# A two-layer encoder trunk on one core: the first norm's scale and offset as rows spread by products, the first loads in another order, and clears on GpSimd

## The chip, the cores and the metric

The kernel runs on one core of one Trainium2 chip, in one launch. The metric is device time in microseconds (us) of that launch, the median of several runs. The engines go by the profile's names: PE (TensorE, with PEld for its weight loads), DVE (VectorE), ACT (ScalarE), POOL (GpSimd) and SP (SyncE, which here only issues DMAs). Each engine takes its own instructions strictly in order and waits on semaphores where an instruction needs another engine's result.

## The reference, cut to what matters

```python
def layer_norm(x, g, b):
    mu = jnp.mean(x, axis=-1, keepdims=True)
    var = jnp.mean(jnp.square(x - mu), axis=-1, keepdims=True)
    return (x - mu) * lax.rsqrt(var + LN_EPS) * g + b

def reference(x, p, ln0_g, ln0_b, w_in, ...):       # x: (1, 512, 1024)
    h = layer_norm(x, ln0_g, ln0_b)                 # the first norm
    for i in range(2):
        u = h @ w_in[i]                             # 1024 -> 2560 columns
        y_hy = hyena_mixer(u[..., :768], ...)       # long convolution
        y_att = diff_attention(u[..., 768:1280], u[..., 1280:1792], u[..., 1792:2304], ...)
        y_pool = pool_mixer(u[..., 2304:], ...)
        mix = jnp.concatenate([y_hy, y_att, y_pool], axis=-1) @ w_out[i]
        h = layer_norm(DN_ALPHA * h + mix, ln1_g[i], ln1_b[i])
        y_moe = hier_moe(h, ...)                    # 16 experts, 2 of them per token
        y_ple = jax.nn.sigmoid(h @ ple_wg[i] + ple_bg[i]) * (p[i] @ ple_wp[i])
        h = layer_norm(DN_ALPHA * h + y_moe + y_ple, ln2_g[i], ln2_b[i])
    return h
```

Only the first norm, the first columns of the first input projection (the query, key and value of attention head 0) and what is loaded or cleared beside them are touched by the change.

## The kernel before, in words

The 512 tokens are four tiles `h[0]` to `h[3]` of 128 tokens by 1024 columns. A tile is normalised in place (`ln`: two passes on DVE, the first subtracts the mean and multiplies by the scale `gb[0]`, the second multiplies by the inverse deviation and adds the offset `gb[1]`), transposed on PE against an identity matrix (`transpose_hl`, eight products `tr` of 128 columns, four to a PSUM bank) and split into a high and a low part, `hT[0]` cast on ACT and `hT[1]` subtracted on DVE (`split`). Weights come from memory as tiles `raw` and are split in the same way into `whi` (ACT) and `wlo` (DVE). Each float32 product is then three PE products, high by high, low by high and high by low (`mm3`, the lines L218 to L220).

The work is written as a list of units (`add`), each with its DMAs, a shape and a generator of PE work. `pump` issues the DMAs of units up to some number ahead and the splits up to another. Units 0 to 3 are the four quarters of attention head 0's weights (`add_head(i, 0, before=...)`); the fourth one's generator runs, tile by tile, norm, transposes and all 24 products `pj` of that tile, then copies the result out of PSUM on ACT (`head_evac`: `uqk`, `uv`). Units 4 and up are the Hyena weights, 512 KB each.

The statistics of tile 0 are taken on DVE (`bn_stats`). Those of tiles 1 to 3 are taken on ACT (`moments`): two passes `lnsq` that sum a half each (L359), a small DVE step `lnneg`, and one pass that squares and sums (L364), after which POOL makes the inverse deviation `lnrs` in two small steps. The first norm pass of a tile overwrites what the squaring pass reads, so it waits for that pass.

The order on each engine is made by a recording layer that places instructions when it expects their inputs; `issue_after(x)` keeps what is issued under it behind instruction `x`, and `behind()` keeps it behind the last norm. Up to eight DMAs of SP are under way at once: the ninth waits for the first.

Of the kernel before, what the change touches and what calls it, by code (L numbers as in the profile page):

```python
# [9 lines left out]
F32 = mybir.dt.float32  # L10
F32R = mybir.dt.float32r
BF16 = mybir.dt.bfloat16
# [9 lines left out]
NT = 4  # L22
# [22 lines left out]
C_N = 818  # L45
# [98 lines left out]
def flat(t):  # L144
    n = len(t.shape) - 1
    if n == 1:
        return t
    letters = " ".join("abcdef"[:n])
    return t.rearrange(f"p {letters} -> p ({letters})")


class Trunk:
# [68 lines left out]

    def split(self, hi, lo, src):

        self.nc.scalar.copy(hi, src)  # L224
        self.nc.vector.tensor_sub(lo, src, hi.bitcast(F32))  # L225


# [160 lines left out]
    def setup(self):  # L388
        nc, A = self.nc, self.A
        cst = self.cst  # L390
        self.ident = cst[:, C_ID:C_ID + 128]
        self.alt = cst[:, C_ALT:C_ALT + 258]
        self.cos = cst[:, C_COS:C_COS + 64].rearrange("p (t d) -> p t d", t=NT)
        self.sin = cst[:, C_SIN:C_SIN + 64].rearrange("p (t d) -> p t d", t=NT)
        self.iota = cst[:, C_IOTA:C_IOTA + 128]
        self.mhalf = self.cp.tile([128, NT], F32, name="mhalf")
        nc.gpsimd.memset(self.mhalf, -0.5)
        self.ones = self.cp.tile([128, 128], F32, name="ones")
        nc.vector.memset(self.ones, 1.0)
        self.tri_b = self.cp.tile([128, 128], BF16, name="tri_b")  # L400
        nc.vector.tensor_copy(self.tri_b, cst[:, C_TRI:C_TRI + 128])
        self.ones_b = self.cp.tile([128, 128], BF16, name="ones_b")
        nc.vector.memset(self.ones_b, 1.0)

        self.qL = self.cp.tile([128, 2, 512], F32R, name="qL")
        nc.vector.memset(flat(self.qL).bitcast(F32), 0.0)

    def setup_late(self):
        nc, A = self.nc, self.A

        vr = self.s2([128, 128], "vr")
        for name, rows in VEC:
            src = A[name]
            nc.sync.dma_start(vr[VOFF[name]:VOFF[name] + rows],
                              bass.AP(tensor=src.tensor, offset=src.offset, ap=[[128, rows], [1, 128]]))
        ps = self.ps("vps")
        nc.tensor.transpose(ps[:, :NVEC], vr[:NVEC], self.ident[:NVEC, :NVEC])
        self.vec = self.cp.tile([128, NVEC], F32, name="vec")
        nc.vector.tensor_copy(self.vec, ps[:, :NVEC])

        self.pw = self.cp.tile([128, DEPTH * 2, 128], F32, name="pw")
        nc.vector.memset(self.pw, 0.0)
        for half in range(2):
            src = A["pool_w"]
            nc.sync.dma_start(
                self.pw[half * 64:half * 64 + 64, :, half * 64:half * 64 + 64],
                bass.AP(tensor=src.tensor, offset=src.offset + half * 4096,
                        ap=[[64, 64], [2 * 4096, DEPTH * 2], [1, 64]]))

        for _ in range(2):  # L430
            x = self.xp.tile([128, 1024], F32, name="xe", tag="xe")
            nc.vector.memset(x, 0.0)

    def lam(self):

        nc, A = self.nc, self.A
        lq = self.s2([128, 2, 2, 2, 64], "lq")
        for n, (a, b) in enumerate((("att_lq1", "att_lk1"), ("att_lq2", "att_lk2"))):
            for o, nm in enumerate((a, b)):
                src = A[nm]  # L440
                nc.sync.dma_start(lq[:, :, n, o], bass.AP(tensor=src.tensor, offset=src.offset,
                                                          ap=[[0, 128], [64, DEPTH], [1, 64]]))
        nc.vector.tensor_mul(lq[:, :, :, 0], lq[:, :, :, 0], lq[:, :, :, 1])
        s = self.sm.tile([128, 2, 2], F32, name="lam_s")
        nc.vector.tensor_reduce(s, lq[:, :, :, 0], axis=AX.X, op=OP.add)
        nc.scalar.activation(s, s, AF.Exp)
        self.nlam = self.cp.tile([128, DEPTH], F32, name="nlam")
        nc.vector.tensor_sub(self.nlam, s[:, :, 1], s[:, :, 0])
        for i in range(DEPTH):
            nc.vector.tensor_scalar(self.nlam[:, i:i + 1], self.nlam[:, i:i + 1], -self.lam_init(i), None, op0=OP.add)  # L450
# [294 lines left out]
    def add_head(self, i, j, before=None):  # L745

        w = self.A["w_in"][i]
        st = {"w": []}

        def mms(ps, t, q, wp):  # L750
            for k in range(2):
                self.mm3(ps[:, :384], [x[:, q * 2 + k, t * 128:(t + 1) * 128] for x in self.hT],
                         [x[:, k] for x in wp], q == 0 and k == 0, q == 3 and k == 1)

        def emit(q):
            def f(wp):
                st["w"].append(wp)
                if before is not None:
                    if q < 3:
                        yield 0.01  # L760
                        return
                    self.new_u()
                    before(0)
                    for t in range(NT):
                        self.stream_tile(self.h[t], self.hT, t)
                        if t + 1 < NT:
                            before(t + 1)
                        ps = self.ps("pj")
                        for n, x in enumerate(st["w"]):
                            mms(ps, t, n, x)  # L770
                        self.head_evac(t, ps)

                        yield 15.36 if t == NT - 1 else 0
                    return
                if q == 0:
                    st["ps"] = [self.ps("pj") for _ in range(NT)]
                if q == 3:
                    self.new_u()
                for t in range(NT):
                    mms(st["ps"][t], t, q, wp)  # L780
                    if q == 3:
                        self.head_evac(t, st["ps"][t])
                    yield 0.96
            return f

        for q in range(4):
            srcs = [((lambda r, s=s: r[:, :, s * 128:(s + 1) * 128]),
                     w[q * 256:(q + 1) * 256, 768 + s * 512 + j * 128:768 + s * 512 + (j + 1) * 128]
                     .rearrange("(k p) n -> p k n", p=128)) for s in range(3)]
            self.add(srcs, [2, 384], emit(q))  # L790

    def new_u(self):
# [217 lines left out]
    def gate_weights(self, i):  # L1010
        nc, A = self.nc, self.A
        raw = self.sm.tile([128, 8, 20], F32, name="gwr", bufs=1)
        nc.sync.dma_start(raw[:, :, 0:4], A["moe_wgc"][i].rearrange("(k p) n -> p k n", p=128))
        nc.sync.dma_start(raw[:, :, 4:20], A["moe_wgf"][i].rearrange("(k p) n -> p k n", p=128))
        gb = self.sm.tile([128, 20], F32, name="gb", bufs=1)
        for src, a, n in ((A["moe_bgc"][i], 0, 4), (A["moe_bgf"][i], 4, 16)):
            nc.sync.dma_start(gb[:, a:a + n], self.row_bcast(src, n))
        gw = self.sm.tile([128, 8, 2, 20], F32R, name="gwhl", bufs=1)
        self.split(gw[:, :, 0], gw[:, :, 1], raw)
        self.gate = gw, gb  # L1020

    def logits(self, half):
# [471 lines left out]
    def start_norm(self, i, t):  # L1494
        if i == 0:
            if t == 0:
                self.ln(self.h[0], self.h[0], self.gb, self.ln_stats(self.h[0]), True)
                self.stats = [None] + [self.ln_stats(self.h[u]) for u in range(1, NT)]
            else:
                with self.behind():  # L1500
                    self.ln(self.h[t], self.h[t], self.gb, self.stats[t])
            self.dump(f"h0_{t}", self.h[t])
        else:
            self.finish(i - 1, t)
# [138 lines left out]
    def build(self):  # L1643
        nc, A = self.nc, self.A
        for i in range(DEPTH):
            self.plan(i)
        self.h = []
        for t in range(NT):
            x = self.s4([128, 1024], "h")
            for cs in (slice(0, 512), slice(512, 1024)) if t == 0 else (slice(0, 1024),):  # L1650
                nc.sync.dma_start(x[:, cs], A["x"][0, t * 128:(t + 1) * 128, cs])
            self.h.append(x)
            if t == 0:
                self.gb = self.gain(A["ln0_g"], A["ln0_b"])
                self.cst = self.cp.tile([128, C_N], F32, name="cst")
                nc.sync.dma_start(self.cst, self.C["cst"])
                self.pump(0, -1)
        self.setup()
        self.hT = self.new_hT()
        self.hd = self.dp.tile([S, 1024], F32, name="hd")  # L1660
        self.yd = self.dp.tile([S, 1024], F32, name="yd")
# [38 lines left out]
```

## Time and profile before

| | |
|---|---|
| median of 3 runs | 1043.53 us (1042.79 to 1048.24) |
| the profiled execution's own time | 1045.37 us |
| its span, first to last instruction | 1043.6 us |
| PE busy | 968.6 us, 93% of the span |
| DVE busy | 779.1 us, 75% |
| ACT busy | 613.6 us, 59% |
| POOL busy | 172.9 us, 17% |

The own time is 1.8 us above the span: that is what lies around the first and last instruction. PE is nearly always busy, except at the very start, so a wait of PE in the first 45 us, where all of the change lies, is what matters; idle time on the other engines costs nothing by itself.

### The profile page before, as it was taken

The page shows a single profiled execution, that of the slowest core. Times are in us where ns is not written, and L with a number is a line of the kernel's source. Part 1 is how long each engine was busy: PE and PEld are TensorE (multiplying, and loading weights), DVE is VectorE, ACT ScalarE, POOL GpSimd, SP SyncE. Part 2 cuts the span into 40 slices and gives each one's busy share as a digit, 9 for nine tenths or more (in the row PEclk, how much of TensorE's full clock was granted, in tenths as well). Part 3 has the DMA queues.
Part 4 walks back from the last instruction along what each step waited for, and adds up shares of the span by engine and source line. Part 5 has one row for each costly group of instructions (what it writes and reads, how often), then busy time and mean ns, then how long its engine had stood idle before and what let it go on. Part 6 is the DMA issues. An engine that isn't in the chain of part 4 may idle for free. (4 is left out here: it accounts for less than half of the span.)

```text
span 1043.6 us, 14416 instructions
## 1 busy us (share of the span) xinstructions
PE 968.6 (93%) x4869; PEld 800.6 (77%) x4870; DVE 779.1 (75%) x1301; ACT 613.6 (59%) x1046; POOL 172.9 (17%) x170
## 2 busy tenths in 40 slices
PE   4999999999989999999979999999998999999995
PEld 3887889898767788777758889898776778877762
DVE  7576897777676778887865578847678587888785
ACT  5425464655653768886843346654655386888673
POOL 1101000000222222422121000000012222333121
PEclk9999999999999999999989999999999999999997
DMA  8816121222974999999974412122186399999974
GB/s 262 239 37 142 51 71 52 71 81 68 316 242 102 306 302 311 307 292 301 285 261 114 109 56 67 51 70 83 61 302 243 94 329 302 315 300 312 293 207 161
DMA packets 156010, 197.49 MB, mean 189 GB/s; under 512 B 20296, under 2 KB 123786, under 8 KB 155925
## 3 DMA queue, kind: packets, MB, share of 16 engines
q1 hardware_dynamic: 135253, 155.58, 45.5%
q0 software_dynamic: 20672, 40.87, 15.1%
q8 instruction: 42, 0.69, 0.3%
q14 instruction: 43, 0.35, 0.1%
HBM read 182.85 MB, written 29.36 MB: 203 GB/s over the span
## 5 line engine op out<-in xcount | busy, mean ns | idle before, releaser
L225 DVE TENSOR_TENSOR wlo<-raw,whi 128x1024 fp32r<-128x1024 f32 (+2 forms) x278 | 324.1, 1182 | 66.0 <-ACT whi L224 61.1
L224 ACT CAST whi<-raw 128x1024 fp32r<-128x1024 f32 (+2 forms) x278 | 277.9, 1024 | 33.1 <-DMA raw<-in_moe_w_dram 13.9
L218 PE MATMUL e<-whi,xT 128*128 128x512 f32 x256 | 106.6, 416 | 2.7 <-ACT xT L224 1.8
L219 PE MATMUL e<-wlo,xT 128*128 128x512 f32 x256 | 103.7, 405 | 0.1
L220 PE MATMUL e<-whi,xT 128*128 128x512 f32 x256 | 101.8, 398 | 0.0
L218 PE MATMUL pj<-whi,hT 128*128 128x384 f32 x256 | 90.0, 352 | 2.3 <-ACT hT L224 1.8
L219 PE MATMUL pj<-wlo,hT 128*128 128x384 f32 x256 | 88.2, 345 | 0.3 <-DVE wlo L225 0.3
L220 PE MATMUL pj<-whi,hT 128*128 128x384 f32 x256 | 87.3, 342 | 0.6 <-DVE hT L225 0.5
L1257 POOL DMA_INDIRECT yd<-ye,rt_tok x28 | 53.1, 1895 | 187.2 <-ACT ye L1323 66.7
L868 ACT ACTIVATE prob<-sc,mx 128x512 f32<-128x512 f32 x64 | 43.7, 688 | 39.1 <-DVE mx L867 36.6
L308 POOL TENSOR_TENSOR ors<-rs_y,mhalf 128x4 f32<-128x4 f32 x8 | 8.5, 1057 | 335.3 <-DVE rs_y L307 335.3
L1251 POOL DMA_INDIRECT xe<-hd,rt_tok x32 | 48.8, 1525 | 91.4 <-PE tr L376 48.1
L218 PEld LDWEIGHTS e<-whi,xT 128*128 128x128 f32 x256 | 48.9, 191 | 12.9 <-ACT xT L224 2.2
L219 PEld LDWEIGHTS e<-wlo,xT 128*128 128x128 f32 x256 | 48.8, 191 | 11.4 <-DVE wlo L225 2.4
L220 PEld LDWEIGHTS e<-whi,xT 128*128 128x128 f32 x256 | 48.8, 191 | 10.0
L219 PE MATMUL e<-wlo,actT 128*128 128x512 f32 x128 | 51.6, 403 | 3.1 <-DVE wlo L225 3.1
L218 PE MATMUL mo<-whi,YT 128*128 128x512 f32 x128 | 53.2, 415 | 0.0
L218 PEld LDWEIGHTS pj<-whi,hT 128*128 128x128 f32 x256 | 48.9, 191 | 4.8 <-ACT hT L224 2.5
L219 PE MATMUL pl<-wlo,hT 128*128 128x512 f32 x128 | 51.4, 401 | 1.1 <-DVE wlo L225 1.1
L218 PE MATMUL pl<-whi,hT 128*128 128x512 f32 x128 | 50.8, 402 | 0.6 <-ACT whi L224 0.5
L218 PE MATMUL e<-whi,actT 128*128 128x512 f32 x128 | 47.8, 398 | 3.8 <-ACT whi L224 2.9
L218 PE MATMUL pj<-hT,whi 128*128 128x512 f32 x128 | 51.2, 404 | 0.0
(340 smaller groups left out, 2313.1 us busy)
## 6 DMA issues: line engine op xcount, KB each, us to landing
raw<-in_moe_w_dram SPq DMA_DIRECT2D x256, 256.0 KB
raw<-in_moe_w_dram SPq DMA_DIRECT2D x64, 512.0 KB
raw<-in_w_in_dram SPq DMA_DIRECT2D x96, 128.0 KB
raw<-in_w_in_dram SPq DMA_DIRECT2D x16, 512.0 KB
raw<-in_ple_wg_dram SPq DMA_DIRECT2D x16, 512.0 KB
raw<-in_w_out_dram SPq DMA_DIRECT2D x14, 512.0 KB
tabi<-c_tabi_dram POOLq DMA_DIRECT2D x8, 516.0 KB, 4.6
tabf<-c_tabf_dram POOLq DMA_DIRECT2D x8, 512.0 KB
```

What stands on the lines that cost most here:

```text
L218: mm(ps, a[0], b[0], start=start, stop=False)
L219: mm(ps, a[0], b[1], start=False, stop=False)
L220: mm(ps, a[1], b[0], start=False, stop=stop)
L224: self.nc.scalar.copy(hi, src)
L225: self.nc.vector.tensor_sub(lo, src, hi.bitcast(F32))
L308: nc.gpsimd.tensor_tensor(out, y, self.mhalf[:, :n], op=OP.pow)
L868: nc.scalar.activation(p[:, c], o, AF.Exp, bias=mx[:, c:c + 1], accum_out=sm[:, c:c + 1])
L1251: self.nc.gpsimd.indirect_dma_start(out=x, out_offset=None, in_=self.hd[:, :], in_offset=bass.IndirectOffsetOnAxis(ap=tok, axis=0), bounds ...
L1257: self.nc.gpsimd.indirect_dma_start(out=self.yd[:, :], out_offset=bass.IndirectOffsetOnAxis(ap=row, axis=0), in_=y, in_offset=None, bounds ...
```

## The change

The scale and the offset of the first norm were two DMAs that each wrote one row of 4 KB to all 128 partitions (512 KB). They are now two DMAs of one row into one partition, and a product of a column of ones with that row, 512 columns at a time, spreads it over the partitions in PSUM; ACT copies the four results to two tiles. Of the constants only the identity (64 KB) is loaded at first. The weights of head 0 are eight DMAs of 192 KB in place of twelve of 128 KB, and all eight stand ahead of tiles 1 to 3 of x. The clears of `qL`, `pw` and two tiles `xe` move from DVE to POOL. The statistics of tiles 1 to 3 and the gate weights' split are kept behind the latest weight cast (`self.cast`).

```diff
     def split(self, hi, lo, src):
-        self.nc.scalar.copy(hi, src)
+        self.cast = self.nc.scalar.copy(hi, src).ins
         self.nc.vector.tensor_sub(lo, src, hi.bitcast(F32))
...
-        self.tri_b = self.cp.tile([128, 128], BF16, name="tri_b")
-        nc.vector.tensor_copy(self.tri_b, cst[:, C_TRI:C_TRI + 128])
-        self.ones_b = self.cp.tile([128, 128], BF16, name="ones_b")
-        nc.vector.memset(self.ones_b, 1.0)
...
-        nc.vector.memset(flat(self.qL).bitcast(F32), 0.0)
+        nc.gpsimd.memset(flat(self.qL).bitcast(F32), 0.0)
...
-        nc.vector.memset(self.pw, 0.0)
+        nc.gpsimd.memset(self.pw, 0.0)
...
-            nc.vector.memset(x, 0.0)
+            nc.gpsimd.memset(x, 0.0)
...
     def lam(self):
+        self.tri_b = self.cp.tile([128, 128], BF16, name="tri_b")
+        with self.behind():
+            nc.vector.tensor_copy(self.tri_b, self.cst[:, C_TRI:C_TRI + 128])
+        self.ones_b = self.cp.tile([128, 128], BF16, name="ones_b")
+        nc.vector.memset(self.ones_b, 1.0)
...
         for q in range(4):
-            srcs = [((lambda r, s=s: r[:, :, s * 128:(s + 1) * 128]),
-                     w[q * 256:(q + 1) * 256, 768 + s * 512 + j * 128:768 + s * 512 + (j + 1) * 128]
-                     .rearrange("(k p) n -> p k n", p=128)) for s in range(3)]
+            srcs = [((lambda r, k=k: r[:, k].rearrange("p (s n) -> p s n", s=3)),
+                     w[q * 256 + k * 128:q * 256 + (k + 1) * 128, 768:2304]
+                     .rearrange("p (s n) -> p s n", s=3)[:, :, j * 128:(j + 1) * 128]) for k in range(2)]
...
-        self.split(gw[:, :, 0], gw[:, :, 1], raw)
+        with self.behind(), self.tc.issue_after(self.cast):
+            self.split(gw[:, :, 0], gw[:, :, 1], raw)
...
                 self.ln(self.h[0], self.h[0], self.gb, self.ln_stats(self.h[0]), True)
-                self.stats = [None] + [self.ln_stats(self.h[u]) for u in range(1, NT)]
+                with self.tc.issue_after(self.cast):
+                    self.stats = [None] + [self.ln_stats(self.h[u]) for u in range(1, NT)]
...
             if t == 0:
-                self.gb = self.gain(A["ln0_g"], A["ln0_b"])
-                self.cst = self.cp.tile([128, C_N], F32, name="cst")
-                nc.sync.dma_start(self.cst, self.C["cst"])
-                self.pump(0, -1)
+                for src in (A["ln0_g"], A["ln0_b"]):
+                    r = self.s4([128, 1024], "grow")
+                    nc.sync.dma_start(r[0:1], bass.AP(tensor=src.tensor, offset=src.offset, ap=[[0, 1], [1, 1024]]))
+                    rows.append(r)
+                nc.sync.dma_start(self.cst[:, :128], self.C["cst"][:, :128])
+                self.pump(3, -1)
+        nc.sync.dma_start(self.cst[:, 128:], self.C["cst"][:, 128:])
         self.setup()
+        self.gb = []
+        for r in rows:
+            g = self.s4([128, 1024], "gain")
+            for c in range(2):
+                cs = slice(c * 512, (c + 1) * 512)
+                ps = self.ps("gb")
+                nc.tensor.matmul(ps, self.ones[0:1], r[0:1, cs], start=True, stop=True)
+                nc.scalar.copy(g[:, cs], ps)
+            self.gb.append(g)
```

What stands where on three engines follows. After line 400 the changed kernel's line numbers are shifted a little (L797 is L798, L1651 is L1657).

ACT before, from its first instruction that needs a result: casts of tile 0's transposes (`hT`) and weights (`whi`), and between them the statistics `lnsq` of tiles 1 to 3.

```order
L224 CAST hT_104<-tr 128x4x128
L224 CAST whi<-raw 128x768
L359 ACTIVATE lnsq,lnsum<-h 128x512 x2
L224 CAST hT_104<-tr 128x4x128
L364 ACTIVATE lnsq,lnvar<-h,lnneg 128x1024
L359 ACTIVATE lnsq,lnsum<-h 128x512 x2
L364 ACTIVATE lnsq,lnvar<-h,lnneg 128x1024
L224 CAST whi<-raw 128x768
```

ACT in the changed kernel, from its first copy on; the 128x1024 casts are the Hyena units 4 and 5, `uqk` is the copy of tile 0's finished products out of PSUM.

```order
L1677 COPY gain<-gb 128x512 x4
L224 CAST whi<-raw 128x768 x2
L224 CAST hT_123<-tr 128x4x128
L224 CAST whi<-raw 128x768
L224 CAST hT_123<-tr 128x4x128
L224 CAST whi<-raw 128x768
L224 CAST whi<-raw 128x1024
L359 ACTIVATE lnsq,lnsum<-h 128x512 x2
L798 COPY uqk<-pj 128x256
L224 CAST whi<-raw 128x1024
L364 ACTIVATE lnsq,lnvar<-h,lnneg 128x1024
```

The squaring pass of tile 1 (L364) stood in fifth place, behind one weight cast; it now stands behind all four casts of head 0's weights, both Hyena casts and the copy `uqk` of tile 0.

DVE in the changed kernel around the norm of tile 0 (`h<-h,lnneg,gain` is the first pass, `h<-h,lnrs,gain` a half of the second) and on to the first pass of tile 1. Before, the half passes stood together, with only the cast of `tri_b` between them.

```order
L334 SCALAR_TENSOR_TENSOR h<-h,lnneg,gain 128x1024
L336 SCALAR_TENSOR_TENSOR h<-h,lnrs,gain 128x512
L225 TENSOR_TENSOR wlo<-raw,whi 128x768
L336 SCALAR_TENSOR_TENSOR h<-h,lnrs,gain 128x512
L225 TENSOR_TENSOR wlo<-raw,whi 128x768
L225 TENSOR_TENSOR hT_124<-tr,hT_123 128x4x128
L225 TENSOR_TENSOR wlo<-raw,whi 128x768
```

A weight split now stands between the two halves of tile 0's second pass: the second half waits for what that split waits for, the first weight cast on ACT.

SP in the changed kernel, from its first issue; the tiles are x (`h`), the rows (`grow`), the constants (`cst`) and the weights (`raw`).

```order
L1657 DMA h<-in_x_dram 128x512 x2
L1662 DMA grow<-in_ln_g_dram 1x1024
L1662 DMA grow<-in_ln_b_dram 1x1024
L1664 DMA cst<-c_cst_dram 128x128
L240 DMA raw<-in_w_in_dram 128x3x128 x8
L1657 DMA h<-in_x_dram 128x1024 x3
L1667 DMA cst<-c_cst_dram 128x690
L421 DMA pw<-in_pool_w_dram 64x4x64 x2
L1014 DMA gwr<-in_moe_wgc_dram 128x8x4
L240 DMA raw<-in_w_in_dram 128x4x256
```

Before, the two 512 KB rows and all constants stood in the places of the short rows and the identity, then one unit of weights, then x, then the other three units. The last row here is Hyena unit 4; unit 5 comes four DMAs later.

## Rows read from the trace of the kernel before

**Rows 1.** The page: busy time of PE, share of the span, count.

```profile
PE 968.6 (93%) x4869; PEld 800.6 (77%) x4870; DVE 779.1 (75%) x1301; ACT 613.6 (59%) x1046; POOL 172.9 (17%) x170
```

**Rows 2.** The timeline of PE: start, us, line, out<-in, count, [idle before it <- releaser].

```profile
11.42 1.95 PE L376 MATMUL tr<-cst,h 128*128 128x128 f32 x8 [11.42 <-DMA cst<-c_cst_dram]
...
15.71 0.52 PE L218 MATMUL pj<-whi,hT 128*128 128x384 f32 x1
...
16.35 0.52 PE L220 MATMUL pj<-whi,hT 128*128 128x384 f32 x1
20.20 0.90 PE L376 MATMUL tr<-cst,h 128*128 128x128 f32 x3 [3.33 <-DVE h L336]
...
25.51 0.34 PE L220 MATMUL pj<-whi,hT 128*128 128x384 f32 x1
25.68 0.34 PE L218 MATMUL pj<-whi,hT 128*128 128x384 f32 x1
...
43.04 0.50 PE L218 MATMUL pj<-hT,whi 128*128 128x512 f32 x1
```

**Rows 3.** Windows: stretch, then us and busy (count) by engine, granted clock, DMA.

```profile
43.00:87.00 44.00, 44.00 (x213) 36.29 (x212) 27.86 (x54) 14.93 (x23) 0.33 (x2) 1.00 0.27 77
...
89.50:94.00 4.50, 4.50 (x16) 3.52 (x17) 3.18 (x15) 2.20 (x7) 3.06 (x5) 0.62 0.20 24
```

**Rows 4.** The timeline of DVE.

```profile
4.37 0.69 DVE L321 BATCH_NORM_STATS2 bnst<-h 128x6 f32<-128x512 f32 x1
5.22 0.91 DVE L432 MEMSET xe<- 128x1024 f32 x1 [0.16 <-issue]
...
8.99 1.28 DVE L334 SCALAR_TENSOR_TENSOR h<-h,lnneg,gain 128x1024 f32<-128x1024 f32 x1 [2.60 <-DMA gain<-in_ln_g_dram]
...
11.45 0.75 DVE L336 SCALAR_TENSOR_TENSOR h<-h,lnrs,gain 128x512 f32<-128x512 f32 x1
...
13.89 0.96 DVE L225 TENSOR_TENSOR wlo<-raw,whi 128x768 fp32r<-128x768 f32 x1
...
16.86 1.28 DVE L334 SCALAR_TENSOR_TENSOR h<-h,lnneg,gain 128x1024 f32<-128x1024 f32 x1 [0.45 <-ACT lnsq L364]
```

**Rows 5.** The timeline of ACT.

```profile
12.54 0.59 ACT L224 CAST hT<-tr 128x512 fp32r<-128x512 f32 x1 [10.49 <-PE tr L376]
13.02 0.83 ACT L224 CAST whi<-raw 128x768 fp32r<-128x768 f32 x1
...
15.58 1.15 ACT L364 ACTIVATE lnsq<-h,lnneg 128x1024 bf16<-128x1024 f32 x1
...
28.17 0.38 ACT L797 COPY uqk<-pj 128x256 f32<-128x256 f32 x1 [1.33 <-PE pj L220]
...
28.59 1.06 ACT L224 CAST whi<-raw 128x1024 fp32r<-128x1024 f32 x1
```

**Rows 6.** The timeline of PE: the one full float32 product of 512 columns there.

```profile
135.59 1.03 PE L734 MATMUL pm<-py,pw 128*128 128x512 f32 x2
```

**Rows 7.** DMA packets of 0 to 20 us, of 15 to 17.5, of 12 to 14.

```profile
DMA packets 4698, 5.43 MB, mean 271 GB/s; under 512 B 320, under 2 KB 3674, under 8 KB 4698
...
DMA packets 1197, 0.64 MB, mean 257 GB/s; under 512 B 78, under 2 KB 1178, under 8 KB 1197
...
DMA packets 299, 0.79 MB, mean 394 GB/s; under 512 B 27, under 2 KB 118, under 8 KB 299
```

**Rows 8.** The timeline of PE behind a wait in the middle of the Hyena part.

```profile
89.50 1.20 PE L636 MATMUL edt<-cst,ed 128*128 128x128 f32 x6 [2.26 <-DVE ed L631]
...
91.78 0.63 PE L220 MATMUL pj<-hT,wlo 128*128 128x512 f32 x1
...
94.07 0.39 PE L220 MATMUL pj<-hT,wlo 128*128 128x512 f32 x1
```

**Rows 9.** The timeline of POOL.

```profile
0.76 0.10 POOL L397 MEMSET mhalf<- 128x4 f32 x1 [0.29 <-POOLq L1686]
...
6.57 0.56 POOL L308 TENSOR_TENSOR lnrs<-rs_y,mhalf 128x1 f32<-128x1 f32 x1
```

More of the change, by code (lines that the diff above doesn't have):

```diff
@@ L1647, in build @@
         self.h = []
+        self.cst = self.cp.tile([128, C_N], F32, name="cst")
+        rows = []
         for t in range(NT):
```

## The prediction, made before the changed kernel had run

> **What bounds the kernel now.** I read the page first: PE is busy 93% of the span [rows 1], so the question is where PE waits and whether the change touches such a wait. Then the windows: from 43 us on PE is busy 44.00 of 44.00 us [rows 3], so whatever time the start gives or takes at 43.04, where the first Hyena product begins [rows 2], is handed on in full. Last the timelines up to that point, one engine at a time.
>
> PE has nothing to do until 11.42, when the constants, and with them the identity, have landed. Tile 0's products then start, and the sixth begins at 16.35. At 20.20 PE resumes, after 3.33 us of waiting for tile 1's norm on DVE [rows 2]. The rows also carry a clock. Two products of 384 columns are 0.64 us apart from 15.71 to 16.35, 0.32 each, and only 0.17 from 25.51 to 25.68: first the pace of the 1.2 GHz level, then that of 2.4 [rows 2]. PE had been idle before both slow stretches.
>
> What delays tile 0 is DVE's wait of 2.60 us for the 512 KB scale, to 8.99 [rows 4]. What delays the rest is ACT, which does casts and statistics in one strict order.
>
> **The change, step by step.** Removed: the 1 MB of broadcast rows, most of the constants ahead of the weights, and 3.2 us of clears on DVE (3,584 columns at 0.91 us per 1,024 [rows 4]). The clears are worth nothing by themselves: DVE ended them early enough to wait 2.60 us for the scale.
>
> *The rows.* They stand where the scale stood on SP, behind x's first tile, whose second half DVE reads at 4.37 without a wait [rows 4]. I let them land at 4.4; the bounds are 4.4 (they queue behind that half) and 9.0 (when the scale itself landed).
>
> *The four products.* They are full float32 products of 512 columns. One, as two records, takes 1.03 us from first start to last end [rows 6]. Behind one another I estimate 0.9: 0.17 for 384 columns makes 0.23 for 512, times four. At the slow pace it is 1.8. PE comes to them from idle, so I take three slow and one fast, 6.3 us; the bounds are 3.6 and 7.2. They end at 10.7.
>
> *The second half of tile 0.* The fourth copy takes 0.59, as the cast of the same shape does, the first weight cast 0.83 [rows 5], its `wlo` 0.96, the half pass 0.75 [rows 4]. They stand in one line because DVE's order now puts `wlo` between the two half passes. Half of the 1.95 us of eight transposes follows [rows 2], 1.0. So 10.7 + 0.6 + 0.8 + 1.0 + 0.75 + 1.0 = 14.8 for the start of tile 0's products; before, the last half pass ended at 12.2 [rows 4]. The early identity thus buys nothing, since the spread products take its place on the path.
>
> *Tile 0.* All four quarters of the weights are loaded by then: 1.57 MB at the 257 GB/s of a stretch that moves almost only 512 B packets [rows 7] are 6.1 us, from 4.4 to 10.5. DVE's three further `wlo` (0.96) and two `hT` (taken as the half pass, 0.75) [rows 4] end near 18.2. PE needs 24 products, 4.1 us fast or 7.7 slow; I take 6.0, so tile 0 ends at 20.8. Before, ACT waited for that end until 28.17 [rows 5]: this part is 7 us better.
>
> *Tile 1.* Here the change takes it back. On ACT the copy `uqk` of tile 0 and Hyena unit 5's cast now stand ahead of tile 1's squaring pass, and tile 1's norm waits for that pass, since it writes over what the pass reads (the wait at 16.86) [rows 4]. So 20.8 + 0.38 + 1.06 + 1.15 [rows 5] = 23.4, two passes of 1.28 [rows 4], and PE transposes tile 1 at 26.0, where it was 20.20. PE idles 5 us in between.
>
> *From there to 43.04.* Before it was 22.84 us for 90 of the 96 products. Now 72 are left, 18 × 0.17 = 3.1 less, so 19.7: 26.0 + 19.7 = 45.7. In both PE begins this stretch slow, so that cancels. The sum is 45.7 − 43.04 = **+2.7 us**.
>
> *At nothing, and what covers it.* GpSimd's clears end before the inverse deviation is wanted at 10.4 (below). The late constants: only `tri_b` on DVE reads them, in the slack before tile 1's statistics. Eight weight DMAs for twelve move the same bytes in the same 512 B pieces. The gate weights' split is wanted only behind the attention. The SP queue: `pw` now waits for a clear on POOL, with the gate weights and Hyena units queued behind it, but SP reaches it only near 10, past the clears.
>
> The profiled execution took 1045.37 us, so its like would take 1048.1; the median of the runs is 1.84 lower, 1043.53 + 2.7 = **1046.2 us**. A measurement of this kernel tells about 0.5% (5.2 us) from no change, so that is inside.
>
> **The rivals.**
>
> *A, the forecast: tile 1 comes late* (0.54). Its own range is +1.5 to +5.2, from the slow or fast products (−2.7, +0.9) and tile 0 (−1.9, +1.7), of which the lower end is cut off as under B.
>
> *B, no difference at all* (0.16). If PE ran fast through the spread products and tile 0, that would end at 16.2. But unit 5's cast also needs its data. By the sizes of the tiles about 5.35 MB stand ahead of or in it, and before 5.43 MB had moved by 20.0 us [rows 7]. So its cast starts near 20.2, tile 1 is transposed at 25.0, and the sum is +1.7. Only if PE's clock also stayed up over that wait would 2.5 us more be saved (as much as the slow rows from 20.20 to 25.5 cost over fast ones [rows 2]): −0.8. Against it stands the wait in front of 89.50: after 2.26 us the products took 0.63 us, at the end 0.39 [rows 8], with a granted clock of 0.62 for that stretch [rows 3]. The Trainium skill (TensorE: Matmul & The Clock Gate, Part 1) says that the gate sets the clock by how busy the array has recently been; the trace agrees at 89.50. By the page the early products should help tile 0 and the idle time after it should undo that for tile 1, which is the order of A. The Trainium skill (DMA: Bandwidth & Descriptors, Specifications) calls 512 B enough for line rate; this trace has 257 GB/s with such packets and 394 with mostly 4 KB ones [rows 7], so here it is not. By the page the weights would take 4 us, unit 5's data would come 2 us sooner, and the sum in B would be that much lower.
>
> *C, faster by over 0.5%* (0.05). The start alone can't give it. The wait of 2.26 us before 89.50 and the slow rows after it (4.5 us at 0.62, 1.7 us lost) would have to go as well; with B that makes −0.8 − 4.0 = −4.8, 1038.7 us, and it would take a little more. Against: DVE's work there follows from PE's products, so both shift together.
>
> *D, slower by over 0.5%* (0.25): GpSimd's clears are slow. They run one after another from 0.87, and the two small steps that give tile 0's inverse deviation stand behind them; the second took 0.56 [rows 9], and I estimate 0.8 for both. The half pass wants it at 10.4, so the clears may take 8.7 us, 2.7 times DVE's 3.2. No wide clear on POOL is in the trace; the bounds are 0.10 us each, as for four columns [rows 9], and no upper one. I take DVE's rate, the nearest by size. At four times it, 12.8 us, the deviation would come at 14.4 and everything 4.0 later: +6.7, 1050.2 us. Rows that land as late as the scale did cost 4.6, 1050.8. The Trainium skill (GPSIMD Engine Reference, Elementwise — side-by-side cycle accounting) gives GpSimd 1.96 times VectorE's time for an addition and advises against moving such work there; no run here shows it. By the page the clears would take an estimated 6.3 us, still under 8.7, and the sum would stay.
>
> **How the numbers follow.** Below −5.2 only C counts, 0.05; above +5.2 D, 0.25; the rest, A and B, 0.70. The range leaves out C and the far end of D, somewhat under 2 in 10: 1042.5 (B, less 0.2) to 1051.5 (D at its two prices, and a little over).
>
> **What would show it.** In the changed profile: rows landing (the first spread product) near 4.4; clears on POOL ended by 9.6; four products ended near 10.7; tile 0's first `pj` near 14.8 and `uqk` waiting for PE until about 21; then, the main thing, PE idle some 5 us before tile 1's transposes at about 26, released by DVE's norm, with slow rows after it; the first Hyena product near 45.7. Wrong would be: tile 1's transposes before 22, or fast rows straight after the wait (B or C); a first half pass that waits for POOL (D); or a first Hyena product at 45.7 and a total that doesn't follow it.

## The result, and the profile of the changed kernel

| | before | changed |
|---|---|---|
| median of 20 runs each, taken together | 1043.57 us (1039.58 to 1048.24) | 1049.99 us (1046.09 to 1057.79) |
| ratio of the times | | 1.0070, 95% interval 1.0057 to 1.0084 |
| the profiled execution's own time | 1045.37 us | 1050.24 us |
| its span | 1043.6 us | 1048.5 us |
| first Hyena product | 43.04 us | 47.67 us |

The change makes the kernel slower, by 6.4 us in the medians and 7.3 us (5.9 to 8.8) by the ratio: more than the 0.5% that can be told from no change, and inside the range given (1042.5 to 1051.5), but not the case that was called likeliest.

The page's first line for the changed kernel answers to [rows 1]. PE's share is the same, but it is busy 5.6 us longer, and its idle time is 74.3 us (1048.5 less 974.2) where it was 75.0 (1043.6 less 968.6). So this line shows no added wait; by itself it would put the loss on the spread products, which are new work. Where the time went has to be read from the timelines and the experiments.

```profile
PE 974.2 (93%) x4877; PEld 804.2 (77%) x4878; DVE 776.1 (74%) x1297; ACT 615.7 (59%) x1050; POOL 174.5 (17%) x174
```

The timeline of PE up to the first Hyena product answers to [rows 2].

```profile
4.22 7.16 PE L1676 MATMUL gb<-grow,ones 1*128 1x512 f32 x8 [4.22 <-DMA grow<-in_ln_g_dram]
...
14.44 1.12 PE L376 MATMUL tr<-cst,h 128*128 128x128 f32 x4 [2.02 <-DVE h L336]
15.21 0.67 PE L218 MATMUL pj<-whi,hT 128*128 128x384 f32 x1
...
18.31 0.52 PE L218 MATMUL pj<-whi,hT 128*128 128x384 f32 x1
18.63 0.44 PE L219 MATMUL pj<-wlo,hT 128*128 128x384 f32 x1
18.91 0.34 PE L220 MATMUL pj<-whi,hT 128*128 128x384 f32 x1
...
21.02 0.33 PE L220 MATMUL pj<-whi,hT 128*128 128x384 f32 x1
27.59 1.97 PE L376 MATMUL tr<-cst,h 128*128 128x128 f32 x8 [6.24 <-DVE h L336]
29.38 0.69 PE L218 MATMUL pj<-whi,hT 128*128 128x384 f32 x1
...
47.67 0.50 PE L218 MATMUL pj<-hT,whi 128*128 128x512 f32 x1
```

Read it from the start: the rows land at 4.22 and the spread products take 7.16 us (eight records, two for each of four products). Tile 0's products begin at 15.21, 0.32 apart until 18.63 and 0.17 apart from 18.91 on. They end at 21.35 (21.02 + 0.33), and then PE has nothing for 6.24 us, until DVE has normalised tile 1. Before, that wait was 3.33 us and ended at 20.20 [rows 2]. The spread products fall into time in which PE used to wait for the constants, until 11.42 [rows 2].

ACT's timeline, which answers to [rows 5], says where the wait comes from.

```profile
11.41 0.58 ACT L1677 COPY gain<-gb 128x512 f32<-128x512 f32 x1 [1.12 <-PE gb L1676]
...
19.57 1.05 ACT L224 CAST whi<-raw 128x1024 fp32r<-128x1024 f32 x1 [2.66 <-DMA raw<-in_w_in_dram]
20.52 0.63 ACT L359 ACTIVATE lnsq<-h 128x512 bf16<-128x512 f32 x1
...
21.76 0.35 ACT L798 COPY uqk<-pj 128x256 f32<-128x256 f32 x1
22.03 1.04 ACT L224 CAST whi<-raw 128x1024 fp32r<-128x1024 f32 x1
22.98 1.14 ACT L364 ACTIVATE lnsq<-h,lnneg 128x1024 bf16<-128x1024 f32 x1
```

ACT stands idle for 2.66 us in front of unit 4's cast, whose data are there at 19.57. Tile 1's two sums come only behind that cast, then `uqk` and unit 5's cast, then the squaring pass at 22.98.

DVE and POOL, behind it, answer to [rows 4] and [rows 9].

```profile
24.25 1.28 DVE L334 SCALAR_TENSOR_TENSOR h<-h,lnneg,gain 128x1024 f32<-128x1024 f32 x1 [2.15 <-ACT lnsq L364]
...
26.25 1.28 DVE L336 SCALAR_TENSOR_TENSOR h<-h,lnrs,gain 128x1024 f32<-128x1024 f32 x1 [0.56 <-POOL lnrs L308]
```

```profile
0.80 0.95 POOL L402 MEMSET qL<- 128x1024 f32 x1
1.69 0.52 POOL L418 MEMSET pw<- 128x512 f32 x1
2.15 1.84 POOL L428 MEMSET xe<- 128x1024 f32 x2
5.48 0.19 POOL L305 TENSOR_SCALAR rs_y<-bnmv 128x1 f32<-128x1 f32 x1 [1.48 <-DVE bnmv L323]
...
24.30 1.28 POOL L305 TENSOR_SCALAR rs_y<-lnvar 128x1 f32<-128x1 f32 x1 [18.00 <-ACT lnsq L364]
25.67 0.55 POOL L308 TENSOR_TENSOR lnrs<-rs_y,mhalf 128x1 f32<-128x1 f32 x1
```

The clears are over at 3.99. For tile 1, DVE's second pass waits another 0.56 us for the inverse deviation: the small step `rs_y`, 0.19 us for tile 0, takes 1.28 us while DVE's first pass runs beside it. That wait isn't new. In the kernel before, tile 1's second pass had it too:

```profile
18.86 1.28 DVE L336 SCALAR_TENSOR_TENSOR h<-h,lnrs,gain 128x1024 f32<-128x1024 f32 x1 [0.57 <-POOL lnrs L308]
```

### The profile page after: what moved, and what is told of

It is laid out like the page before. It is cut to its first block, busy times and chain, and to the rows that moved or that the text cites. A ratio compares the mean times of both kernels' runs of the same rounds, so it can differ in the third digit from the quotient of the medians.

```text
span 1048.5 us, 14369 instructions
## 1 busy us (share of the span) xinstructions
PE 974.2 (93%) x4877; PEld 804.2 (77%) x4878; DVE 776.1 (74%) x1297; ACT 615.7 (59%) x1050; POOL 174.5 (17%) x174
## 5 line engine op out<-in xcount | busy, mean ns | idle before, releaser
L224 ACT CAST whi<-raw 128x1024 fp32r<-128x1024 f32 (+2 forms) x278 | 277.3, 1024 | 28.1 <-DMA raw<-in_moe_w_dram 10.2
L1253 POOL DMA_INDIRECT xe<-hd,rt_tok x32 | 46.7, 1459 | 89.8 <-PE tr L376 46.7
L218 PE MATMUL pl<-whi,hT 128*128 128x512 f32 x128 | 51.6, 408 | 1.8 <-ACT whi L224 1.8
L220 PE MATMUL pl<-whi,hT 128*128 128x512 f32 x128 | 51.5, 403 | 0.0
```

Source lines behind the costliest of these rows:

```text
L218: mm(ps, a[0], b[0], start=start, stop=False)
L220: mm(ps, a[1], b[0], start=False, stop=stop)
L224: self.cast = self.nc.scalar.copy(hi, src).ins
L1253: self.nc.gpsimd.indirect_dma_start(out=x, out_offset=None, in_=self.hd[:, :], in_offset=bass.IndirectOffsetOnAxis(ap=tok, axis=0), bounds ...
```

## The experiments

Theory T: tile 1's norm is late because its statistics stand on ACT behind unit 4's cast, with its data, and behind `uqk` and unit 5's cast. Rival R: the four spread products make tile 0 late and all else follows. Rival Q: x's tiles are late because the weights are loaded ahead of them. Theory F, added later, says that small loads delay unit 4's data.

The first four ran side by side (before: 1042.68 us).

**e1, the statistics no longer held back.**

```diff
-                with self.tc.issue_after(self.cast):
+                with contextlib.nullcontext():
                     self.stats = [None] + [self.ln_stats(self.h[u]) for u in range(1, NT)]
```

The new first line is an empty context, which holds nothing back.

> The changed kernel, but the statistics of tiles 1 to 3 are no longer kept behind the latest weight cast; all else as changed. ACT's order then has tile 1's two sums behind the first of the four head casts and its squaring pass ahead of the fourth, and Hyena unit 5's cast behind all three squaring passes. Theory T (tile 1 is late because its statistics stand on ACT behind unit 4's cast, which waits for its data until 19.57, and behind uqk and unit 5's cast): tile 1's transposes near 22 in place of 27.59, first Hyena product near 44.5 in place of 47.67, median about 1047 (-3). Rival R (the four spread products, 7.16 us, make tile 0 late and all that follows): they are untouched, so 27.6, 47.7 and 1050 stay. Rival Q (x's tiles come too late because the weights' DMAs stand ahead of them): the sums would wait for the DMA of tile 1 and its transposes would not come before 25.

Measured: 1047.10 us, ratio 1.0036 (1.0021 to 1.0052). PE's timeline:

```profile
19.13 0.69 PE L220 MATMUL pj<-whi,hT 128*128 128x384 f32 x1 [2.15 <-DVE hT L225]
...
23.38 1.97 PE L376 MATMUL tr<-cst,h 128*128 128x128 f32 x8 [0.68 <-DVE h L336]
...
44.36 0.50 PE L218 MATMUL pj<-hT,whi 128*128 128x512 f32 x1
```

As T expected, with the spread products untouched: 44.36 where 44.5 was given; tile 1's transposes came at 23.38, later than the 22 given, but far from R's 27.6. R falls. Part of what is left of the loss sits in tile 0 now: its products stop for 2.15 us in front of 19.13. DVE's timeline says why:

```profile
17.38 0.23 DVE L435 CAST tri_b<-cst 128x128 bf16<-128x128 f32 x1 [2.42 <-DMA cst<-c_cst_dram]
```

The cast of `tri_b` now stands in front of tile 0's last splits, and DVE waits 2.42 us for the late constants. Tile 1's first sum waited 0.89 us for x; that this reached the path isn't shown, so Q has a small part at most.

**e2, casts one unit ahead at the start.**

```diff
-        self.ahead_raw, self.ahead_split, self.cap = 4, 2, 1 << 30
+        self.ahead_raw, self.ahead_split, self.cap = 4, 1, 1 << 30
```

> The changed kernel with one number changed: casts are issued one unit ahead and not two at the start, so the latest cast behind which the statistics are kept is that of the fourth head quarter, not that of Hyena unit 4. T: ACT goes from that cast (ended at 16.9) straight to tile 1's sums and squaring pass, tile 1's transposes near 22.5; but the sums of tiles 2 and 3 now stand ahead of tile 1's hT cast, some 2.5 us of wait behind the transposes; first Hyena product near 46.0, median about 1048.3 (-1.7). R: no difference, 27.6, 47.7 and 1050.

Measured: 1046.64 us, ratio 1.0028 (1.0013 to 1.0043).

```profile
22.98 1.10 PE L376 MATMUL tr<-cst,h 128*128 128x128 f32 x8 [1.90 <-DVE h L336]
25.32 0.69 PE L218 MATMUL pj<-whi,hT 128*128 128x384 f32 x1 [1.24 <-ACT hT L224]
...
45.48 0.50 PE L218 MATMUL pj<-hT,whi 128*128 128x512 f32 x1
```

One number, which moves unit 4's cast behind tile 1's statistics and `uqk`, brings tile 1 forward by 4.6 us. Work for later tiles then stands ahead of tile 1's `hT` cast, as expected, and costs 1.24 us where some 2.5 were given.

**e3, the rows issued first.** The loop that loads the two rows stands ahead of x's first tile; nothing else moves on any engine.

```diff
         rows = []
+        for src in (A["ln0_g"], A["ln0_b"]):
...
         for t in range(NT):
             x = self.s4([128, 1024], "h")
...
-                for src in (A["ln0_g"], A["ln0_b"]):
```

> The changed kernel with the two 4 KB rows issued ahead of x's first tile; every engine's order is otherwise the same. The first spread product should start near 2.6 in place of 4.22 and tile 0's products near 13.6 in place of 15.21. R: everything behind follows by the same 1.6 us: tile 1's transposes near 26.0, first Hyena product near 46.1, median -1.6. T: unit 4's data, not tile 0, releases ACT at 19.57, so tile 1's transposes come at most 0.7 us earlier (27.0 to 27.6), the longer wait of PE in front of them takes up the rest, median -0.7 or none.

Measured: 1050.70 us, ratio 1.0063 (1.0040 to 1.0086). The rows of PE, then of ACT:

```profile
2.39 7.16 PE L1676 MATMUL gb<-grow,ones 1*128 1x512 f32 x8 [2.39 <-DMA grow<-in_ln_g_dram]
...
28.30 1.97 PE L376 MATMUL tr<-cst,h 128*128 128x128 f32 x8 [8.28 <-DVE h L336]
...
47.68 0.50 PE L218 MATMUL pj<-hT,whi 128*128 128x512 f32 x1
```

```profile
19.82 1.04 ACT L224 CAST whi<-raw 128x1024 fp32r<-128x1024 f32 x1 [4.74 <-DMA raw<-in_w_in_dram]
```

This is the cleanest separation. The spread products and tile 0's start are 1.8 us earlier, tile 0's end 1.3; the wait in front of tile 1 grows from 6.24 to 8.28 us, and the first Hyena product stays where it was. Tile 0 doesn't release tile 1; unit 4's data do. T had allowed 27.0 to 27.6 for tile 1's transposes, and they came at 28.30: unit 4's data were 0.25 us later, and unit 5's cast waited 0.37 us for its own. The slow rows behind ended sooner, so the two cancelled.

**e4, the kernel before with the statistics held back.**

```diff
-        self.nc.scalar.copy(hi, src)
+        self.cast = self.nc.scalar.copy(hi, src).ins
...
-                self.stats = [None] + [self.ln_stats(self.h[u]) for u in range(1, NT)]
+                with self.tc.issue_after(self.cast):
+                    self.stats = [None] + [self.ln_stats(self.h[u]) for u in range(1, NT)]
```

> The kernel before with one part of the change alone: the statistics of tiles 1 to 3 are kept behind the latest weight cast (that of Hyena unit 4). Rows, products, loads and clears are as before. T: this alone makes it slower by about what the whole change did or more, since the weights land later here: tile 1's transposes near 30 in place of 20.20, first Hyena product near 50 in place of 43.04, median about 1050.7 (+7). R: no spread product is in it, so 43.0 and 1043.5 stay.

Measured: 1050.71 us, ratio 1.0069 (1.0043 to 1.0095). PE's timeline:

```profile
29.32 1.97 PE L376 MATMUL tr<-cst,h 128*128 128x128 f32 x8 [5.87 <-DVE h L336]
...
50.07 0.50 PE L218 MATMUL pj<-hT,whi 128*128 128x512 f32 x1
```

T had given near 30, near 50 and about 1050.7. This part alone, in the kernel before, costs as much as the whole change.

The next four ran side by side (before: 1043.89 us).

**e5, the kernel before with the rows and the spread products alone.** The lines of the change that load the two rows and spread them replace `self.gain`; the rest is before's code.

```diff
-                self.gb = self.gain(A["ln0_g"], A["ln0_b"])
+                for src in (A["ln0_g"], A["ln0_b"]):
+                    r = self.s4([128, 1024], "grow")
...
+                nc.tensor.matmul(ps, self.ones[0:1], r[0:1, cs], start=True, stop=True)
+                nc.scalar.copy(g[:, cs], ps)
```

> The kernel before with the rows and the four spread products alone in place of the two broadcast DMAs; loads, identity, statistics and clears are otherwise before's code. The order written for SP follows: the gate's small loads and the pool weights now stand ahead of units 1 to 3 of the head. T: the products cost nothing by themselves, since tile 1's statistics keep their early place on ACT; first Hyena product between 41 and 44 (before: 43.04), median 1041.5 to 1043.5. R: 7.16 us of products in front of tile 0 show, first Hyena product at 46 or later, median 1046 or more. If it is slower with tile 1's statistics early, the weights behind the small loads must be what is waited for: ACT's second to fourth head casts would then wait for their DMA beyond 18.

Measured: 1044.77 us, ratio 1.0004 (0.9986 to 1.0022), first Hyena product at 42.91. Four products of 7.16 us in front of tile 0 make no difference that shows (1.5 us less to 2.3 more, by the interval), in place of 1 MB of broadcast rows. The start is as T gave it; the median is 1.3 us above T's range and below R's 1046.

**e6, the gate's small loads held back.**

```diff
         raw = self.sm.tile([128, 8, 20], F32, name="gwr", bufs=1)
+        if i == 0:
+            nc.gpsimd.tensor_copy(raw[:, 0, 0:1], self.stats[3][1])
+            nc.gpsimd.tensor_copy(raw[:, 0, 4:5], self.stats[3][1])
```

> The changed kernel with the two small gate loads (16 and 64 byte pieces, 80 KB) held back until tile 3's statistics are done, by two tiny copies on GpSimd that write where the loads land; before, they were issued behind Hyena unit 4, in the changed kernel ahead of and behind it at 11.4 and 13.7. Theory F (added to T: what sets unit 4's 19.57 is these small pieces, 217 and 135 GB/s from 16 to 20 us): unit 4's cast starts near 17.5, tile 1's transposes near 25.5 in place of 27.59, first Hyena product near 45.7, median -2 (1048). T without F: unit 4's data come at 19.5 as before, 27.6, 47.7, no difference.

Measured: 1049.01 us, ratio 1.0038 (1.0016 to 1.0059). First two windows of the changed kernel, then the second of them in e6 (the last three numbers are the granted clock, the DMA engines' busy share and GB/s), then ACT and PE of e6:

```profile
16.00:18.00 2.00, 2.00 (x8) 2.00 (x8) 2.00 (x3) 0.91 (x2) 0.00 (x0) 1.00 1.16 217
18.00:20.00 2.00, 2.00 (x11) 2.00 (x11) 0.32 (x2) 0.43 (x1) 0.00 (x0) 1.00 0.73 135
```

```profile
18.00:20.00 2.00, 2.00 (x13) 2.00 (x12) 0.45 (x2) 0.73 (x1) 0.00 (x0) 1.00 1.10 347
```

```profile
19.27 1.05 ACT L224 CAST whi<-raw 128x1024 fp32r<-128x1024 f32 x1 [2.24 <-DMA raw<-in_w_in_dram]
```

```profile
26.46 1.97 PE L376 MATMUL tr<-cst,h 128*128 128x128 f32 x8 [5.70 <-DVE h L336]
...
34.30 0.41 PE L218 MATMUL pj<-whi,hT 128*128 128x384 f32 x1
...
48.13 0.50 PE L218 MATMUL pj<-hT,whi 128*128 128x512 f32 x1
```

F falls: far more bytes move, but unit 4's cast starts only 0.3 us earlier. What does set the time of unit 4's data stays open. Tile 1 comes 1.1 us sooner (its squaring pass stands ahead of unit 5's cast here), and even that is lost: the slow rows, 0.32 apart, last from 28.7 to 34.3, where in the changed kernel they were over at 32.6.

**e7 and e8, meant to beat both.** Casts one unit ahead at the start as in e2, with the statistics of tile t + 1 issued behind tile t - 1's `hT` casts; the cast of `tri_b` behind the norms; rows first as in e3, gate loads as in e6; and in the loop of the spread products:

```diff
-                nc.scalar.copy(g[:, cs], ps)
+                last = nc.scalar.copy(g[:, cs], ps).ins
+                n += 1
+                with self.tc.issue_after(last):
+                    self.pump(3, n - 1 - 0)
```

e8 has `n - 1 - 1` in the last line.

> A version meant to beat both: the changed kernel with the rows issued first, a head cast behind each of the four copies of the spread products (the first quarter's cast ahead of the second copy), casts one unit ahead at the start, tile 1's statistics behind the last head cast and those of tiles 2 and 3 each behind hT casts of the tiles before, gate loads held as in the run before, tri_b behind the norms. T: tile 0's products near 13, tile 1's transposes at or below 20.5 with under 1 us of idle PE in front, first Hyena product near 39.5 (before: 43.04), median near 1039.5. R: with the products as slow as ever no version of the change is below 1043. If the first quarter's data land after 5.5, the copies wait behind its cast, and all of it is up to 1.5 us later.

> As the run before, but each head cast one copy later (the first quarter's behind the second copy). T: first Hyena product near 40.5, median near 1040.5; it is the better of the two only if the first quarter's data land after the first copy has ended.

Measured: e7 1044.51 us, ratio 1.0005 (0.9987 to 1.0023), first Hyena product at 40.25; e8 1044.22 us, 0.9997 (0.9981 to 1.0013), at 41.09. In e7 the first head cast waited for its data until 7.76 and the copies behind it too, as the expectation allowed. Both take back the whole loss of the change; that either is faster than the kernel before can't be shown, and the medians given, near 1039.5 and 1040.5, were missed by 5.0 and 3.7 us.

The last three with times ran side by side (before: 1043.19 us). They ask why the medians seemed to exceed the shift of the first Hyena product.

**e9, e10 and e11, the parts that reach past the start.** e9 is the kernel before with two edits of the change alone: two DMAs in place of three for each head quarter, and the gate's split behind the latest cast. e10 is the changed kernel, and e11 is e7, with the same two undone. In e9:

```diff
-            srcs = [((lambda r, s=s: r[:, :, s * 128:(s + 1) * 128]),
...
+            srcs = [((lambda r, k=k: r[:, k].rearrange("p (s n) -> p s n", s=3)),
...
-        self.split(gw[:, :, 0], gw[:, :, 1], raw)
+        with self.behind(), self.tc.issue_after(self.cast):
+            self.split(gw[:, :, 0], gw[:, :, 1], raw)
```

> The kernel before with the two parts of the change that reach past the start: each head quarter's weights as two DMAs of 192 KB in place of three of 128 KB (all heads of both layers), and the gate weights' split kept behind the latest cast. All else as before. These two alone move a few instructions later in the program (some products of mo, sc and pl on PE, the gate's split on ACT and DVE of layer 1). Theory L (the 2 to 3 us by which the medians of the changed kernel and of three of its variants exceed the shift of the first Hyena product in their traces come from these later moves): median 1.5 to 3 us above before, plus whatever the first Hyena product moves. Theory N (they are the scatter of runs, and of the slow stretches of TensorE's clock that fall now here, now there): median within 1 us of before plus the shift of the first Hyena product.

> The changed kernel with the same two parts undone (three DMAs of 128 KB for each quarter, gate split as before); the order behind the start is then that of before. The start stays late by theory T: tile 1's transposes near 27, first Hyena product 4 to 5 us later than before. L: median 4 to 5 above before. N: 6 to 7 above before, as the changed kernel.

> The version of e7 with the same two parts undone. In e7 the first Hyena product came 2.8 us sooner than before, and the median did not follow (+0.5). L: it now follows, first Hyena product near 40 and median 2.5 to 4 below before, faster than both kernels. N: median within 1.5 of before again, whatever the start shows.

Measured: e9 1046.17 us, ratio 1.0030 (1.0010 to 1.0050), first Hyena product at 41.93; e10 1051.57 us, 1.0100 (1.0066 to 1.0134), at 50.94; e11 1044.94 us, 1.0017 (0.9996 to 1.0038), at 43.47. L would make e9 slower, which it is, and e10 and e11 better, which they aren't; N would leave e9's median within 1 us of before plus its shift, and it is 3 us up. Neither is shown. Both forecasts for the starts missed: e10's first Hyena product was to come 4 to 5 us after 43.04 and came 7.9 after, and e11's was to come near 40. ACT's timeline of e10 with PE's row for tile 1 behind it, then ACT's of e11, show that the two edits do matter at the start of these kernels:

```profile
21.99 0.33 ACT L224 CAST gwhl<-gwr 128x160 fp32r<-128x160 f32 x1 [5.23 <-DMA gwr<-in_moe_wgf_dram]
22.22 1.04 ACT L224 CAST whi<-raw 128x1024 fp32r<-128x1024 f32 x1
```

```profile
29.40 1.97 PE L376 MATMUL tr<-cst,h 128*128 128x128 f32 x8 [7.62 <-DVE h L336]
```

```profile
9.45 0.83 ACT L224 CAST whi<-raw 128x768 fp32r<-128x768 f32 x1 [1.08 <-DMA raw<-in_w_in_dram]
...
13.57 0.83 ACT L224 CAST whi<-raw 128x768 fp32r<-128x768 f32 x1 [1.30 <-DMA raw<-in_w_in_dram]
```

Without its hold the gate's split stands in front of unit 4's cast and makes ACT wait 5.23 us for 64 KB in small pieces; tile 1 comes 1.8 us later than in the changed kernel. With three DMAs for each quarter the casts wait for data again, and tile 0's products in e11 start 1.8 us later than in e7 (16.71 against 14.94). The rest of e10's and e11's later starts, some 1.5 us each, is slow rows of PE that last longer.

**e12, the kernel before once more, unchanged.**

> The kernel before, once more, unchanged, for a second profile. Over the eleven kernels and the changed one, the median's shift exceeds that of the first Hyena product by 1.7 us on the mean. If that common part comes from the one profile of before that all are read against, its first Hyena product stands 1 to 2 us earlier here (41 to 42), or its slow stretches of PE behind 60 us add up to less; if both profiles agree within 0.5 us (42.5 to 43.5), the common part is not in the reading of the start and stays open.

Measured, one run: 1042.61 us (another beside it 1039.56). PE's timeline:

```profile
10.46 1.94 PE L376 MATMUL tr<-cst,h 128*128 128x128 f32 x8 [10.46 <-DMA cst<-c_cst_dram]
...
41.88 0.50 PE L218 MATMUL pj<-hT,whi 128*128 128x512 f32 x1
```

That is inside the 41 to 42 given. The constants landed at 10.46, as in e4 (10.45) and e9 (10.44) with the same first loads; in the profile that the prediction read it was 11.42 [rows 2]. By three profiles against one, 43.04 was late, and 41.88 is the better base. Against it:

| kernel | shift of first Hyena product, us | ratio of times, as us |
|---|---|---|
| changed | +5.8 | +7.3 (5.9 to 8.8) |
| e1, e2, e3 | +2.5, +3.6, +5.8 | +3.8, +2.9, +6.6 |
| e4, e5, e6 | +8.2, +1.0, +6.3 | +7.2, +0.4, +4.0 |
| e7, e8 | -1.6, -0.8 | +0.5, -0.3 |
| e9, e10, e11 | +0.1, +9.1, +1.6 | +3.1, +10.4, +1.8 |

The right column is the ratio less 1, times 1043 us. The two agree within 2.3 us but for e9, 0.5 us apart on the mean. One reason why single readings differ is that slow stretches of PE fall in different places. Here are 4.2 us from the same place in the work, of the changed kernel and of the kernel before (the granted clock is the third number from the end):

```profile
120.50:124.70 4.20, 4.15 (x20) 3.96 (x21) 2.96 (x5) 1.47 (x3) 0.00 (x0) 0.59 0.40 129
```

```profile
116.20:120.40 4.20, 4.16 (x32) 3.97 (x33) 3.63 (x7) 1.46 (x3) 0.00 (x0) 1.00 0.39 129
```

At a granted clock of 0.59, most of it at the lower of the two levels (1.2 GHz), 20 products are done where 32 were. Why e9's median is 3 us up while its start is not stays open.

## Why the prediction was right in its mechanism and wrong in size

*Bound and place.* Right. PE's time after the first Hyena product is handed on nearly unchanged: 43.04 to 66.44 us for the next landmark, the first `fps` product, in the kernel before, 47.67 to 71.05 in the changed one.

*The rows* were given 4.4 and landed at 4.22; the last of *the four products* was given 10.7 and ended at 11.38. The estimate of three slow ones and a fast one was wrong: all four ran slow, at the upper bound of 7.2.

*The second half of tile 0* was given 14.8 and came at 15.21, by the line of steps that was written down. *Tile 0's end*, given 20.8, came at 21.35. It was about right and didn't matter.

*Tile 1* is the step that failed. Its direction was right: its norm waits for ACT, and PE idles (5 us given, 6.24 measured). But the sum hung on tile 0's end and `uqk`. In fact ACT waited for unit 4's data until 19.57, did that cast and tile 1's sums, and reached `uqk` at 21.76, when PE had been done for 0.4 us; e3 shows that an earlier tile 0 changes nothing. That a sum hung on the wrong releaser came so near is luck: the two chains happened to end 0.4 us apart. The prediction knew a wait for weights' data, but put it at unit 5 and only under rival B. The chain in figures: the squaring pass was to end at 23.4, and DVE started at 24.25 (+0.85); the two passes were to take 2.6 us and took 3.34 (+0.75), since POOL's inverse deviation, which had no term, came late. The rows that were read already had those 3.34 us, from tile 1's first pass at 16.86 [rows 4] to its transposes at 20.20 [rows 2]. So 27.59 in place of 26.0, 1.6 us.

*From there to 43.04* was given 19.7 us and took 20.08 (+0.4). That both kernels begin slow and that this cancels was right; e6 shows it needn't be.

*The base.* The sum was made against a first Hyena product of 43.04, read from one profile in which the constants had landed 1.0 us later than in three others. 2.7 + 1.6 + 0.4 + 1.1 (43.04 - 41.88 = 1.16) = 5.8, which is the shift against e12, and 6.4 is the difference of the medians. The prediction subtracted a fixed 1.84 from the profiled time to come to the median, as if the start that it read were typical.

*At nothing.* The clears were hidden, as said. The Trainium skill (GPSIMD Engine Reference, Elementwise — side-by-side cycle accounting) gives GpSimd 1.96 times VectorE's time for an addition. A clear of 1,024 columns took 0.95 us here, against 0.91 on DVE [rows 4], so the factor doesn't carry over to a clear. The two DMAs for each quarter and the held gate split were booked at nothing. Without them the first Hyena product comes 3.3 us later in the changed kernel (e10) and 3.2 us later in e7's version (e11), of which 1.8 us each are waits and the rest slow rows; put into the kernel before, they leave the start where it was (e9, 41.93). The late constants cost nothing in the changed kernel, as said, but 2.42 us of DVE's time in e1, where the slack that hid them is gone.

*The rivals.* D, which carried the chance of slower by over 0.5%, was wrong in both its forms (clears ended at 3.99, rows landed at 4.22): the outcome came out of A, whose range ended at +5.2. The range of the forecast reached to 1051.5 for the prices of D, so that it holds 1049.99 is in part luck. B was wrong, since the clock did not stay up over the wait: behind the 6.24 us in which PE had nothing, the granted clock is 0.50, the lower of the two levels (again the third number from the end).

```profile
28.00:32.00 4.00, 3.87 (x16) 3.15 (x15) 3.68 (x5) 2.89 (x8) 2.46 (x4) 0.50 0.30 88
```

C did not come.

## What to carry to other kernels

When work is held behind "the latest" instruction of an in-order engine, ask which one that is and what it waits for: here a cast for the next stage, whose data were still on the way, stood in front of the statistics that the critical tile needed. Follow such a chain from each input that it has, data included, and take the latest; the step that looks like the natural releaser may have slack (e3 settled that by moving two small loads). And before a sum of a few us is read against one profile, see from a second one how much its start moves by itself.

## What the runs showed of the hardware that was not expected

The same loads landed 1.0 us apart in executions of one kernel (10.46 and 11.42). The slow pace of the first products does not stand in the clock column: the changed kernel's window of 16 to 18 us, shown under e6, has a granted clock of 1.00, though its rows are 0.32 apart until 18.63 and 0.17 from 18.91. The same pace does stand in it from 28 to 32 us, as 0.50. A one-column step on POOL took 0.19 us alone and 1.28 us beside a DVE pass. Raising the DMA rate from 135 to 347 GB/s in a stretch brought the one load that was waited for only 0.3 us forward.
